# A decoder trunk step on one core: x loaded ahead of c on two queues, the first norm's copy and scale moved, first weight chunks of four tiles

## The chip, the cores and the metric

The kernel runs on one core of one Trainium2 chip. The metric is device time in microseconds (us) of one execution. Before the change it is 1359.24 us, the median of three runs (1358.83 to 1359.36).

## The reference

One step of one decoder layer, for two request groups that share the weights: a prompt of 256 tokens and 8 samples of 4 tokens, together 288 columns (N in the kernel). The width is 2048, so x is 16 tiles of 128 rows by 288 columns. Cut to what matters here:

```
mod = silu(c) @ w_ada + b_ada                  # 6 x 2048 values for each of 9 conditions (1 prompt, 8 samples)
sh1, sc1, g1, sh2, sc2, g2 = split(mod, 6)
h = rmsnorm(x, norm1) * (1 + sc1) + sh1        # rmsnorm: x * rsqrt(mean(x*x) + eps) * g
proj = h @ w_in                                # one input projection for both mixers
...                                            # pooling mixer, Mamba-2 mixer, output projection, gated residual
h2 = rmsnorm(x, norm2) * (1 + sc2) + sh2
ffn = (silu(conv(h2 @ w_gate)) * (h2 @ w_val)) @ w_down
y = rmsnorm(x + g2 * ffn, norm_f)
```

Everything is in float32. The change touches what stands ahead of the input projection and its first chunks: the loads of x and c, the first norm, its modulation and the first weights.

## The kernel before, in words

Features lie on the partitions and the 288 tokens along the free axis. Each large product is done in three matmuls for each weight tile and operand tile (`mm3`, L293): the weight is split into a rounded part `whi` (an ACT cast, L281) and its remainder `wlo` (a VectorE subtraction, L283), the operand likewise into `h1h` and `h1l` (L445, L446), and three of the four cross products are summed. Weights come from one long array, `wflat`, in chunks of up to 1024 columns, in the order in which they are needed. They land in 16 raw buffers (8 + 8); split weights have two buffers of each kind while the input projection begins (SPLIT0, SPLIT1, one each).

The order of work at the start:

- SP issues DMAs in the order c (L182), the four tiles of x (`xa`, L483, four feature tiles each), the first four modulation weights (`raw_ada`, L262), then the first two projection chunks (`raw_xbc`, L924), then further weights as `top_up` asks for them (L269). ACT issues the small constants `early` (L184). DMAs share eight completion semaphores in turn, so each DMA issue first waits for the one eight before it.
- ACT takes silu of c into `sc_c` (L202), for which it first loads a table, then loads the table of the square root by a dummy operation (`warm`, L909).
- The squares of x are taken by ACT (xa0, xa2, L915) and VectorE (xa1, xa3, L917), into a tile with two buffers, and summed over the partitions on TensorE (`ssum`, L919). After each sum two matmuls on the same square tile keep TensorE busy (`warm_pe`, L220 and L921); 14 such matmuls on a tile of ones stand at the very start (L910). From L908 to L945 a manager (`in_order`, L205) pins each of the three engines to the order in which the program names the operations.
- `sqs` (L926) copies the sums out; `rstd_of` (L238) makes the reciprocal root and spreads it over all partitions by a matmul into PSUM (`pbrstd`, L248), and copies that into SBUF (`rstd`, L253). Between these steps run the modulation's matmuls for feature tile 0 (`ada_group_units`, L344), with their copy (`asb`, L329), transpose (L383) and additions (L394, L339).
- `modulate_steps` (L424) makes the projection's operand: x times the norm (L428, from PSUM for feature tile 0, from the SBUF copy for the others), then scale and shift of the prompt's 256 columns (on VectorE at L436, or on ACT at L434 if `act` is set) and of the samples' 32 columns (L441, L442), then cast and remainder (L445, L446).
- The projection runs in seven blocks (BLOCKS, L45), each a range of feature tiles (k) and of output tiles (m). Block 0 is feature tile 0 with all 28 output tiles. `_xbc_chunks` (L79) cuts a block's weights: for block 0 the first chunk has 4 output tiles, the next three have 8. The first two are split by hand ahead of the block (L936 to L943); the third is split by hand and pinned at output tile 3 (L1013), the fourth in `xbc_units` (L621) when it is reached. Each output tile's sum is copied out by ACT or VectorE (L642).

Outside of the pinned parts a scheduler orders each engine's instructions at build time.

Of the kernel before, what the change touches and what calls it, by code (L numbers as in the profile page):

```python
# [14 lines left out]
AF = mybir.ActivationFunctionType  # L15
# [3 lines left out]
P = 128  # L19
D = 2048  # L20
# [4 lines left out]
N = NP + NS  # L25
NC9 = 1 + NB
# [35 lines left out]
KGROUPS = [(0, 1), (1, 1), (2, 2), (4, 4), (8, 4), (12, 4)]  # L62
# [4 lines left out]
RAWC = 1024  # L67
# [11 lines left out]
def _xbc_chunks(bi):  # L79
    (k0, gk), (a, b) = BLOCKS[bi]  # L80
    mper = RAWC // (gk * P)
    cuts = [a, *range(a + (mper // 2 if bi == 0 else mper), b, mper), b]
    return [(list(range(k0, k0 + gk)), list(range(m, n))) for m, n in zip(cuts, cuts[1:])]


# [76 lines left out]
def kernel(ctx: ExitStack, tc, ins, outs):  # L162
    nc = tc.nc
# [13 lines left out]
    def aux(name):  # L177
        return px.tile([P, 512], F32, tag="aux", name=name)


    ct = kp.tile([P, KT, NC9], F32, tag="asb", name="ct")
    nc.sync.dma_start(ct, ins["c"])  # L182
    early = kp.tile([P, NE], F32, name="early")
    nc.scalar.dma_start(early, ins["early"])  # L184
    vec = kp.tile([P, NV], F32, name="vec")
    ident = early[:, K_ID:K_ID + P]
    tri = vec[:, K_TRI:K_TRI + P]
# [11 lines left out]
    bada = early[:, V_BADA:V_BADA + 96].rearrange("p (a k) -> p a k", a=6)  # L199
    sc_c = kp.tile([P, KT, 32], F32, name="sc_c")  # L200
    nc.vector.memset(sc_c, 0.0)
    nc.scalar.activation(sc_c[:, :, 0:NC9], ct, AF.Silu)  # L202

    @contextmanager
    def in_order(*engines):  # L205
# [14 lines left out]
    def warm_pe(n, rhs=None):  # L220

        for _ in range(n):
            nc.tensor.matmul(wps[:, :P], ones, ones if rhs is None else rhs, start=True, stop=True)
# [11 lines left out]
            nc.tensor.matmul(ps[:, c:c + 1], src[:, a:a + P], rhs, start=first and c == 0, stop=last,  # L235
                             skip_group_check=True)

    def rstd_of(ps, n, name, keep=True, mid=None):  # L238

        r3 = kp.tile([P, 3], F32, tag="r3", name="r3" + name)  # L240
        nc.scalar.activation(r3, ps[:, 0:3], AF.Sqrt, bias=epst[:, 0:1], scale=1.0 / n)
        nc.vector.reciprocal(r3, r3)
        if mid:
            mid()
        pb = aux("pb" + name)
        for c, a in enumerate((0, P, N - P)):
            n0 = max(a, c * P)
            nc.tensor.matmul(pb[:, n0:a + P], r3[:, c:c + 1].to_broadcast([P, P]), ident[:, n0 - a:],  # L248
                             start=True, stop=True)
        if not keep:  # L250
            return pb[:, :N], None
        r = kp.tile([P, N], F32, tag="rstd", name=name)
        nc.scalar.copy(r, pb[:, :N])  # L253
        return pb[:, :N], r

# [20 lines left out]
    def fetch(key):  # L276
        return ahead.pop(key)[1]

    def split_steps(raw, a, n, name):
        hi = wp[0].tile([P, RAWC], F32R, tag="whi", name="whi_" + name)  # L280
        yield nc.scalar.copy(hi[:, :n], raw[:, a:a + n])  # L281
        lo = wp[0].tile([P, RAWC], F32R, tag="wlo", name="wlo_" + name)
        yield hi, lo, nc.vector.tensor_tensor(lo[:, :n], raw[:, a:a + n], hi[:, :n].bitcast(F32), ALU.subtract)  # L283

    def split(raw, a, n, name, urgent=True, pin=False):
        with tc.high_priority() if urgent else nullcontext():
            cast, (hi, lo, rest) = split_steps(raw, a, n, name)
        if pin:
            tc.keep_in_program_order(cast)
            tc.keep_in_program_order(rest)  # L290
        return hi, lo
# [7 lines left out]
    ready = {}  # L299
# [124 lines left out]
    def modulate_steps(xv, rstd, which, shp, k0, gk, name, eng=None, act=False):  # L424

        h = kp.tile([P, 4, N], F32, tag="hmod", name="h_" + name, bufs=2)
        hv = h[:, :gk, :]
        nc.vector.tensor_tensor(hv, xv,  # L428
                                rstd.unsqueeze(1).to_broadcast([P, gk, N]), ALU.mult)
        yield  # L430
        for i in range(gk):
            am, sh = amul[:, which, k0 + i, 0:1], ada[:, shp, k0 + i, 0:1]
            if act:
                nc.scalar.activation(h[:, i, 0:NP], h[:, i, 0:NP], AF.Identity, bias=sh, scale=am)  # L434
            else:
                nc.vector.tensor_scalar(h[:, i, 0:NP], h[:, i, 0:NP], am, sh, ALU.mult, ALU.add)  # L436
        hs = hv[:, :, NP:N].rearrange("p k (b l) -> p k b l", b=NB)
        sa = amul[:, which, k0:k0 + gk, 1:NC9].unsqueeze(3).to_broadcast([P, gk, NB, NL])
        sb = ada[:, shp, k0:k0 + gk, 1:NC9].unsqueeze(3).to_broadcast([P, gk, NB, NL])
        eng = eng or nc.gpsimd  # L440
        eng.tensor_tensor(hs, hs, sa, ALU.mult)  # L441
        eng.tensor_tensor(hs, hs, sb, ALU.add)  # L442
        yield
        for i in range(gk):
            nc.scalar.copy(xhi[0][k0 + i], h[:, i, :])  # L445
            nc.vector.tensor_tensor(xlo[0][k0 + i], h[:, i, :], xhi[0][k0 + i].bitcast(F32), ALU.subtract)  # L446
# [33 lines left out]
    xa = []  # L480
    for q in range(4):
        t = mx.tile([P, 4, N], F32, tag="blk", name=f"xa{q}", bufs=4)
        nc.sync.dma_start(t, ins["x"][:, 4 * q:4 * q + 4, :])  # L483
        xa.append(t)

    def xav(k0, gk):
        return xa[k0 // 4][:, k0 % 4:k0 % 4 + gk, :]
# [165 lines left out]
    def drain(gen):  # L653
        for _ in gen:
            pass
# [252 lines left out]
    with in_order(*(e.engine for e in (nc.tensor, nc.scalar, nc.vector))):  # L908
        nc.scalar.activation(warm, sc_c[:, 0, 0:1], AF.Sqrt, scale=0.0)  # L909
        warm_pe(WU[0])  # L910
        ssum = aux("ssum1")
        for q in range(4):
            sq = kp.tile([P, 4, N], F32, tag="hmod", name=f"sq{q}", bufs=2)
            if q % 2 == 0:
                nc.scalar.activation(sq, xa[q], AF.Square)  # L915
            else:
                nc.vector.tensor_tensor(sq, xa[q], xa[q], ALU.mult)  # L917
            for i in range(4):
                nc.tensor.matmul(ssum[32 * i:32 * i + 32, :N], ones[:, 0:32], sq[:, i, :],  # L919
                                 start=(q == 0), stop=(q == 3), tile_position=(0, 32 * i))  # L920
            warm_pe(WU[1], sq[:, 0, 0:P])  # L921
        cond = ada_group_units(0)
        next(cond)
        first = [load(("xbc", 0, ci)) for ci in range(2)]  # L924
        sqs = kp.tile([P, N], F32, tag="xsq", name="sqs", bufs=2)
        nc.vector.tensor_copy(sqs, ssum[:, :N])  # L926
        next(cond)
        ssum = aux("ssum1b")
        col_sums(ssum, sqs, early[:, K_S4:K_S4 + 1], True, True)
        next(cond)  # L930
        rstd1p, rstd1 = rstd_of(ssum, D, "rstd1", mid=lambda: (next(cond), next(cond)))
        mod = modulate_steps(xav(0, KGROUPS[0][1]), rstd1p, 0, 0, 0, KGROUPS[0][1], "g0", nc.vector)
        next(mod)
        next(cond)
        drain(cond)
        parts = [split_steps(t, 0, len(ms) * P, f"xbc0_{i}") for i, (t, (_, ms)) in  # L936
                 enumerate(zip(first, _xbc_chunks(0)))]
        for p in parts:
            next(p)
        next(mod)  # L940
        ready["xbc", 0, 0] = next(parts[0])[:2]
        drain(mod)
        ready["xbc", 0, 1] = next(parts[1])[:2]  # L943
        mod = modulate_steps(xav(*KGROUPS[1]), rstd1, 0, 0, *KGROUPS[1], "g1", nc.vector, True)
        next(mod)  # L945
# [46 lines left out]
    for bi in range(len(BLOCKS)):  # L992
        last = bi + 1 == len(BLOCKS)
        top_up()
        if last:

            wp[0].drop(w0)
            w0_ctx.close()
            sx[0] = mx_ctx.enter_context(tc.tile_pool(name="sx", bufs=1, reuse_waits="tile"))
            hi, lo = split(load(("dt",)), 0, KT * NH, "dt")  # L1000
            ps = pm.tile([P, 512], F32, tag="mm", name="mm_dt")
            for k in range(KT):
                mm3(ps[0:NH, :N], hi, lo, k, xhi[0][k], xlo[0][k], k == 0, k == KT - 1, NH)
            late_states()
            dt_stage(ps)
        elif bi == 4:
            nc.sync.dma_start(vec, ins["vec"])
        elif bi == 5:
            late_loads()
        for i, m in enumerate(xbc_units(bi)):  # L1010
            if not last:
                top_up()
                if (bi, i) == (0, 3):  # L1013
                    ready["xbc", 0, 2] = split(fetch(("xbc", 0, 2)), 0, RAWC, "xbc0_2", pin=True)
                if i in VIS[bi]:
                    next(nxt)
                    top_up()
            else:
                pull(back, 0.5 if m < 20 else RB1) if m >= 9 else None
                pull(adas, RA1 / AY)  # L1020

    late = {}
    n = 0
# [44 lines left out]
    x = ff.tile([P, KT, N], F32, name="x")  # L1068
# [342 lines left out]
```

## Time and profile before

| what | before |
|---|---|
| median of three runs | 1359.24 us |
| the profiled execution: its own time | 1359.61 us |
| its span in the profile | 1357.8 us |
| TensorE matmuls busy | 1342.5 us, 99% |
| VectorE / ScalarE / GpSimd busy | 60% / 43% / 16% |
| mean DMA rate over the span | 238 GB/s |

Times in the profile count from the start of the span. PE is TensorE, PEld its weight loads, DVE VectorE, ACT ScalarE, POOL GpSimd, SP SyncE; SPq and ACTq are their sequencers issuing DMAs. In the rows in order of time the columns are the start, the duration, the engine, the line of the program, the operation with its output and inputs, the count, and in brackets the idle time before it and what ended it. A row of waits gives who waited for whom, then us in total, times, and the longest. A row of stretches gives the stretch, its length, the busy time (and instructions) of PE, PEld, DVE, ACT and POOL, the granted TensorE clock, the DMA share and GB/s. A row of DMA issues gives the count, KB each and the median us to landing. TensorE's weight load and matmul rows of a float32 product appear twice for each matmul.

### The profile page before, as it was taken

How to read it: one execution, taken by the hardware profiler on the slowest of the kernel's cores; microseconds unless marked ns; L12 is line 12 of the kernel's file. 1: busy time of each engine (PE TensorE's matmuls, PEld its weight loads, DVE VectorE, ACT ScalarE, POOL GpSimd, SP SyncE). 2: the span in 40 equal slices, each digit the busy share in tenths (PEclk: the TensorE clock that was granted, in tenths of full speed). 3: DMA queues.
4: the chain of work that ended last, by engine and by line, in shares of the span. 5: the costliest groups of instructions: out<-in, count | busy, mean ns of one | idle time of the engine just before them, and what ended most of it. 6: DMA issues, size and time to landing. Idle time of an engine off the chain costs nothing.

```text
span 1357.8 us, 26226 instructions
## 1 busy us (share of the span) xinstructions
PE 1342.5 (99%) x10557; PEld 1247.4 (92%) x10557; DVE 810.1 (60%) x1349; ACT 578.6 (43%) x908; POOL 221.0 (16%) x428
## 2 busy tenths in 40 slices
PE   9999999999999999999999999999999999999997
PEld 7889988776779889999999999999999999999996
DVE  5775568778564448645565455656654556566543
ACT  5243234587643335534443334443433344434442
POOL 0000002122221213111221001212220011222221
PEclk9999999999999999999999999999999999999998
DMA  9999668877888877777555455555554555555531
GB/s 378 405 408 355 252 216 323 335 263 288 326 302 334 310 265 257 248 293 265 184 182 184 167 176 185 197 193 182 189 178 167 183 191 185 192 200 194 180 117 71
DMA packets 97338, 323.20 MB, mean 238 GB/s; under 512 B 10752, under 2 KB 19904, under 8 KB 97216
## 3 DMA queue, kind: packets, MB, share of 16 engines
q1 hardware_dynamic: 93312, 310.64, 62.8%
q0 software_dynamic: 3184, 9.69, 1.9%
q8 instruction: 83, 1.36, 0.4%
q10 hardware_dynamic: 720, 1.19, 0.2%
q14 instruction: 39, 0.32, 0.1%
HBM read 309.78 MB, written 10.39 MB: 236 GB/s over the span
## 4 chain that ended last, share of the span: by engine, by line
PE 96%; DVE 2%; DMA 1%; ACT 0%; issue 0%; SPq 0%; POOL 0%; DVEq 0%; POOLq 0%; ACTq 0%
PE mm_down L296 7%; PE mm_down L295 7%; PE mm_down L297 7%; PE mm_val L296 6%; PE mm_gate L296 6%; PE mm_gate L295 6%; PE mm_gate L297 6%; PE mm_val L297 6%; PE mm_val L295 6%; PE xbc L295 5%; PE adap L324 5%; PE xbc L296 4%; PE xbc L297 4%; PE mm_out L295 3%; PE mm_out L296 3%; PE mm_out L297 2%
## 5 line engine op out<-in xcount | busy, mean ns | idle before, releaser
L296 PE MATMUL mm_down<-al,whi_down 128*128 128x288 f32 x688 | 202.9, 295 | 0.0
L295 PE MATMUL mm_down<-ah,whi_down 128*128 128x288 f32 x688 | 202.7, 295 | 0.0
L297 PE MATMUL mm_down<-ah,wlo_down 128*128 128x288 f32 x688 | 202.4, 294 | 0.0
L296 PE MATMUL mm_gate<-h2l,whi_gate 128*128 128x288 f32 x640 | 189.1, 296 | 0.0
L296 PE MATMUL mm_val<-h2l,whi_val 128*128 128x288 f32 x640 | 189.1, 295 | 0.0
L297 PE MATMUL mm_val<-h2h,wlo_val 128*128 128x288 f32 x640 | 188.8, 295 | 0.0
L297 PE MATMUL mm_gate<-h2h,wlo_gate 128*128 128x288 f32 x640 | 188.8, 295 | 0.0
L295 PE MATMUL mm_gate<-h2h,whi_gate 128*128 128x288 f32 x640 | 188.7, 295 | 0.0
L295 PE MATMUL mm_val<-h2h,whi_val 128*128 128x288 f32 x640 | 187.9, 294 | 0.0
L283 DVE TENSOR_TENSOR wlo_gate<-raw_gate,whi_gate 128x1024 fp32r<-128x1024 f32 x80 | 97.8, 1225 | 135.4 <-ACT whi_gate L281 135.2
L283 DVE TENSOR_TENSOR wlo_down<-raw_down,whi_down 128x1024 fp32r<-128x1024 f32 x96 | 107.5, 1119 | 116.1 <-ACT whi_down L281 115.0
L281 ACT CAST whi_down<-raw_down 128x1024 fp32r<-128x1024 f32 x96 | 92.4, 962 | 167.3 <-PE mm_down L296 118.0
L281 ACT CAST whi_gate<-raw_gate 128x1024 fp32r<-128x1024 f32 x80 | 83.9, 1051 | 159.5 <-PE mm_gate L296 67.7
L281 ACT CAST whi_val<-raw_val 128x1024 fp32r<-128x1024 f32 x80 | 84.1, 1051 | 126.0 <-issue 103.1
L295 PE MATMUL xbc<-h1h,whi_xbc 128*128 128x288 f32 x448 | 133.0, 301 | 1.2 <-ACT h1h L445 1.2
L296 PE MATMUL xbc<-h1l,whi_xbc 128*128 128x288 f32 x448 | 132.1, 296 | 0.0
L297 PE MATMUL xbc<-h1h,wlo_xbc 128*128 128x288 f32 x448 | 130.8, 297 | 0.0
L295 PEld LDWEIGHTS mm_down<-ah,whi_down 128*128 128x128 f32 x688 | 129.3, 188 | 0.0
L296 PEld LDWEIGHTS mm_down<-al,whi_down 128*128 128x128 f32 x688 | 129.3, 188 | 0.0
L297 PEld LDWEIGHTS mm_down<-ah,wlo_down 128*128 128x128 f32 x688 | 129.1, 188 | 0.0
L295 PEld LDWEIGHTS mm_gate<-h2h,whi_gate 128*128 128x128 f32 x640 | 120.5, 188 | 5.0 <-ACT ah L1176 3.4
L295 PEld LDWEIGHTS mm_val<-h2h,whi_val 128*128 128x128 f32 x640 | 120.5, 188 | 0.0
(323 smaller groups left out, 2979.3 us busy)
## 6 DMA issues: line engine op xcount, KB each, us to landing
raw_adap<-wflat SPq DMA_DIRECT2D x128, 512.0 KB, 5.5
raw_gate<-wflat SPq DMA_DIRECT2D x80, 512.0 KB, 3.5
raw_val<-wflat SPq DMA_DIRECT2D x80, 512.0 KB, 3.6
raw_ada<-wflat SPq DMA_DIRECT2D x64, 512.0 KB, 9.7
raw_xbc<-wflat SPq DMA_DIRECT2D x51, 512.0 KB, 8.9
raw_down<-wflat SPq DMA_DIRECT2D x48, 512.0 KB, 3.5
raw_out<-wflat SPq DMA_DIRECT2D x32, 512.0 KB, 6.6
raw_down<-wflat SPq DMA_DIRECT2D x32, 384.0 KB, 3.0
```

What stands on the lines that cost most here:

```text
L281: yield nc.scalar.copy(hi[:, :n], raw[:, a:a + n])
L283: yield hi, lo, nc.vector.tensor_tensor(lo[:, :n], raw[:, a:a + n], hi[:, :n].bitcast(F32), ALU.subtract)
L295: nc.tensor.matmul(ps, whi[:, w], bh, start=first, stop=False)
L296: nc.tensor.matmul(ps, whi[:, w], bl, start=False, stop=False)
L297: nc.tensor.matmul(ps, wlo[:, w], bh, start=False, stop=last)
L324: nc.tensor.matmul(ps[32 * j:32 * j + 32, :nb], sc_c[:, k, :], raw[:, c:c + nb], start=(k == 0), stop=(k == KT - 1), tile_position=(0, 32 ...
```

## The change

- The tiles of x are loaded first, xa0 and xa2 by SP and xa1 and xa3 by ACT; the loads of c and of `early` and the silu of c are written behind them.
- The first norm's copy to SBUF is written behind feature tile 0's cast and remainder; until then its PSUM form alone is used.
- For feature tile 0, ACT scales and shifts the prompt's columns instead of VectorE.
- Block 0's weights are cut into chunks of 4, 4, 4, 8 and 8 output tiles instead of 4, 8, 8 and 8; the third, fourth and fifth are split by hand and pinned at output tiles 3, 7 and 13.

```
 def _xbc_chunks(bi):
-    cuts = [a, *range(a + (mper // 2 if bi == 0 else mper), b, mper), b]
+    cuts = [a, *([4, 8] if bi == 0 else []), *range(a + (12 if bi == 0 else mper), b, mper), b]
...
-    nc.sync.dma_start(ct, ins["c"])
-    nc.scalar.dma_start(early, ins["early"])
...
-    nc.scalar.activation(sc_c[:, :, 0:NC9], ct, AF.Silu)
...
-    def rstd_of(ps, n, name, keep=True, mid=None):
+    def rstd_of(ps, n, name, keep=True, mid=None, later=False):
...
         r = kp.tile([P, N], F32, tag="rstd", name=name)
+        if later:
+            return pb[:, :N], lambda: (nc.scalar.copy(r, pb[:, :N]), r)[1]
         nc.scalar.copy(r, pb[:, :N])
...
-        nc.sync.dma_start(t, ins["x"][:, 4 * q:4 * q + 4, :])
+        (nc.scalar if q % 2 else nc.sync).dma_start(t, ins["x"][:, 4 * q:4 * q + 4, :])
         xa.append(t)
+    nc.sync.dma_start(ct, ins["c"])
+    nc.scalar.dma_start(early, ins["early"])
+    nc.scalar.activation(sc_c[:, :, 0:NC9], ct, AF.Silu)
...
-        rstd1p, rstd1 = rstd_of(ssum, D, "rstd1", mid=lambda: (next(cond), next(cond)))
-        mod = modulate_steps(xav(0, KGROUPS[0][1]), rstd1p, 0, 0, 0, KGROUPS[0][1], "g0", nc.vector)
+        rstd1p, rstd1 = rstd_of(ssum, D, "rstd1", mid=lambda: (next(cond), next(cond)), later=True)
+        mod = modulate_steps(xav(0, KGROUPS[0][1]), rstd1p, 0, 0, 0, KGROUPS[0][1], "g0", nc.vector, True)
...
         ready["xbc", 0, 0] = next(parts[0])[:2]
         drain(mod)
+        rstd1 = rstd1()
...
-                if (bi, i) == (0, 3):
-                    ready["xbc", 0, 2] = split(fetch(("xbc", 0, 2)), 0, RAWC, "xbc0_2", pin=True)
+                if bi == 0 and i in (3, 7, 13):
+                    ci = {3: 2, 7: 3, 13: 4}[i]
+                    ready["xbc", 0, ci] = split(fetch(("xbc", 0, ci)), 0, len(_xbc_chunks(0)[ci][1]) * P,
+                                                f"xbc0_{ci}", pin=True)
```

As built, ACT still issues the load of `early` ahead of its two tiles of x.

## The prediction

> **What bounds the kernel now.** I read the page first (busy times, then the chain that ended last), then TensorE's waits, then the instructions in order of time over the first 20 us.
>
> ```profile
> span 1357.8 us, 26226 instructions
> PE 1342.5 (99%) x10557; PEld 1247.4 (92%) x10557; DVE 810.1 (60%) x1349; ACT 578.6 (43%) x908; POOL 221.0 (16%) x428
> PE 96%; DVE 2%; DMA 1%; ACT 0%; issue 0%; SPq 0%; POOL 0%; DVEq 0%; POOLq 0%; ACTq 0%
> ...
> PE xbc L295 <- ACT h1h L445: 1.2, 2, 0.9
> ...
> PE pool L877 <- DVE pout L872: 0.7, 1, 0.7
> ```
>
> TensorE is busy 99% of the span and holds 96% of the chain. The two wait rows are the largest of two stretches, 19 to 200 us and from there to the end: after the first projection matmul TensorE hardly waits, and never for a DMA. So whatever moves that first matmul moves the end by the same amount; no slack behind it can take up a delay, and a DMA that runs further ahead buys nothing. The question is when the first projection matmul starts. Before, that is 19.22 us, and these rows lead to it (start, duration, engine, what it waited for):
>
> ```profile
> 3.03 1.28 ACT L202 ACT_TABLE_LOAD   x1 [3.03 <-DMA ct<-c]
> 4.33 0.34 ACT L202 ACTIVATE sc_c<-ct 128x144 f32<-128x144 f32 x1
> 4.68 1.28 ACT L909 ACT_TABLE_LOAD   x1
> 5.97 0.20 ACT L909 ACTIVATE warm<-sc_c 128x1 f32<-128x1 f32 x1
> 6.08 1.15 ACT L915 ACTIVATE sq<-xa 128x1152 f32<-128x1152 f32 x1
> 8.78 1.16 ACT L915 ACTIVATE sq<-xa 128x1152 f32<-128x1152 f32 x1 [1.55 <-DMA xa<-x]
> ...
> 7.29 1.36 DVE L917 TENSOR_TENSOR sq<-xa 128x1152 f32<-128x1152 f32 x1 [5.57 <-DMA xa<-x]
> 10.24 1.36 DVE L917 TENSOR_TENSOR sq<-xa 128x1152 f32<-128x1152 f32 x1 [1.59 <-DMA xa<-x]
> 12.41 0.46 DVE L926 COPY sqs<-ssum 128x288 f32<-128x288 f32 x1 [0.81 <-PE ssum L919]
> ...
> 7.28 0.69 PE L919 MATMUL ssum<-sq,ones 128*32 128x288 f32 x8 [0.59 <-ACT sq L915]
> 9.99 0.69 PE L919 MATMUL ssum<-sq,ones 128*32 128x288 f32 x8
> 10.62 0.71 PE L223 MATMUL warm<-sq,ones 128*128 128x128 f32 x4
> 11.65 0.69 PE L919 MATMUL ssum<-sq,ones 128*32 128x288 f32 x8 [0.32 <-DVE sq L917]
> 19.22 0.80 PE L295 MATMUL xbc<-h1h,whi_xbc 128*128 128x288 f32 x4 [0.86 <-ACT h1h L445]
> ```
>
> Two things are to be seen. The x tiles land at 7.29, 8.78 and 10.24 us, and squares and sums follow them. And ACT's first square stands behind four instructions, the first of which, a table load, waits for c: from c at 3.03 to the square at 6.08 it is **3.05 us**. Before, this hides behind the transfer of the first x tile.
>
> **The change part by part.**
>
> *Loading x ahead of c.* In the list of the changed kernel as built, SP issues xa0, xa2, then c, then the weights; ACT issues early (still first), xa1, xa3. ACT's order behind that is unchanged: table load (waiting for c's DMA), silu, table load, warm, square of xa0, square of xa2. So ACT's squares now wait for a c that stands behind two tiles on its own queue. When does it land?
>
> ```profile
> GB/s 0 0 176 272 209 412 393 393 424 430 399 428 418 415 415 415 415 415 385 421 396 399 426 399 382 415 426 393 410 421 404 399 431 399 393 431 415 393 432 393
> ...
> xa<-x SPq DMA_DIRECT2D x4, 576.0 KB, 6.1
> early<-early ACTq DMA_DIRECT2D x1, 152.5 KB, 2.4
> ct<-c SPq DMA_DIRECT2D x1, 72.0 KB, 2.2
> ```
>
> The first row is the rate in slices of 0.75 us: from 3.75 us on, one queue alone moves about 410 GB/s, the plateau that lasts. If SP's queue were served first, c would land when two tiles, c and early have passed, the bytes behind the landing at 7.29; if ACT's tiles all pass too, 10.24. Large tiles first may also spare part of the slow start: the slices of 176, 272 and 209 lose (236+140+203)/412 x 0.75 = 1.05 us against 412. With two queues side by side, c is nearly the last of the five: I take **9.5 us** (10.24 less half of that loss and a little), ends 7.3 and 10.2.
>
> The Trainium skill, page "DMA: Bandwidth & Descriptors", sections "Queues, rings and completion order" and "Rules for kernel authors", speaks against this step: engines take packets in turn from the queues with work, each queue in its own order, and spreading loads over SP and ACT saves issue time, not bandwidth. By that rule c lands beside xa3, near the upper end, and the sum would be up to 0.7 us larger; the plateau on one queue agrees with it.
>
> ACT then: 9.5 + 3.05 = 12.55, first square to 13.7, and the first sum on TensorE starts at 13.75 instead of 7.28. The two extra DMA issues on ACT, and SP's two fewer, are hidden in ACT's wait.
>
> *What waits behind it.* TensorE runs the sums in order, and the square tile has two buffers: the square of xa2 waits until sum and warm matmuls of xa0 are done, that of xa3 (VectorE) for those of xa1. Before, loads spaced these out; now they make a staircase. And TensorE stands idle from the end of its first warm matmuls to 13.75:
>
> ```profile
> 1.06 5.63 PE L223 MATMUL warm<-ones 128*128 128x128 f32 x28 [1.06 <-DVE ones L192]
> ...
> 2.71 1.70 PE L223 MATMUL warm<-ones 128*128 128x128 f32 x7
> ...
> 5.70 0.99 PE L223 MATMUL warm<-ones 128*128 128x128 f32 x7
> ...
> 1347.15 0.85 PE L248 MATMUL pbrstdf<-early,r3rstdf 128*128 128x128 f32 x6
> ...
> 1350.00:1350.40 0.40, 0.00 (x0) 0.00 (x0) 0.40 (x2) 0.00 (x0) 0.00 (x0) 1.00 0.74 242
> 1350.40:1350.70 0.30, 0.00 (x0) 0.00 (x0) 0.30 (x2) 0.00 (x0) 0.00 (x0) 0.89 0.07 19
> 1350.70:1351.00 0.30, 0.00 (x0) 0.00 (x0) 0.30 (x2) 0.00 (x0) 0.00 (x0) 0.50 0.37 131
> ```
>
> Seven warm matmul rows take 1.70 us early and 0.99 us from 5.70 on: TensorE starts slow and is quick some 4.6 us after its first matmul. After the last one (ended 1348.0) the granted clock, the third figure from the right, falls from 1.00 to 0.50 at about 1350.6, 2.6 us later. The idle time now is 13.75 - 6.69 = 7.1 us, so TensorE should come back slow, by 1.70/0.99 = 1.7, until about 13.75 + 4.6 = 18.35. A sum with its warm matmuls takes 10.62 + 0.71 - 9.99 = 1.34 us quick, 2.2 slow.
>
> The Trainium skill, page "TensorE: Matmul & The Clock Gate", Part 1, has the clock halve after an idle window of about 3.4 us and return after a busy one, counted freely. By that rule the return comes 3.4 to 6.8 us after the restart, which makes the sum up to 1 us smaller or larger; the fall after 2.6 us agrees with halving, and is a little earlier.
>
> The staircase, slow: xa0's sum and warm 13.75 to 15.95; xa1's (its square long done) to 18.15; xa2's (square 16.0 to 17.15) mostly quick, 18.15 to 19.5; square of xa3 18.2 to 19.55, sum from 19.6; the copy of the sums, which came 0.76 after that sum began (12.41 - 11.65), at 20.35. Before: 12.41. **+7.9 us.**
>
> *The norm's copy and the scale on ACT.* From the sums' copy to the first projection matmul it is 6.81 us before:
>
> ```profile
> 15.29 0.38 PEld L370 LDWEIGHTS adag<-raw_ada,sc_c 128*32 128x32 f32 x16 [0.23 <-DMA raw_ada<-wflat]
> ...
> 15.87 0.85 PE L248 MATMUL pbrstd<-early,r3rstd 128*128 128x128 f32 x6
> ...
> 17.19 0.45 DVE L428 TENSOR_TENSOR h_g<-xa,pbrstd 128x288 f32<-128x288 f32 x1 [2.36 <-ACT rstd L253]
> 17.76 0.17 DVE L339 SCALAR_TENSOR_TENSOR amul<-ada,early 128x9 f32<-128x9 f32 x1
> 18.74 0.43 ACT L445 CAST h1h<-h_g 128x288 fp32r<-128x288 f32 x1
> L434 ACT ACTIVATE h_g<-h_g,ada,amul x15: 586/588/604, 31.7 to 177.9; 128x256 f32<-128x256 f32 x15
> ```
>
> Three waits shrink. The modulation's weights will long have landed: -0.23. The multiply at 17.19 waited for ACT's copy of the norm; in the list of the changed kernel it waits for the norm's matmuls alone, which end at 15.87 + 0.85 = 16.72: -0.45. From amul to the cast took 0.98 us (17.76 to 18.74) over VectorE's scale and two small operations; now ACT scales (0.59) beside those two, 0.2 + 0.59 = 0.79: -0.2. Together **-0.9 us**. The copy moved behind the first cast delays only later copies, which wait for the projection's first sums a microsecond later anyway; were that cover gone it would cost its 0.40. ACT's casts of the first two weight chunks stand ahead of the scale, and are smaller now; they fit behind the modulation's copy.
>
> *Chunks of four tiles.* Bytes and matmuls stay. But there are two buffers of split weights, so the third chunk's cast (ACT) and remainder (VectorE) must fit behind the tiles of the second.
>
> ```profile
> 19.86 0.29 PE L296 MATMUL xbc<-h1l,whi_xbc 128*128 128x288 f32 x1
> 19.99 0.30 PE L297 MATMUL xbc<-h1h,wlo_xbc 128*128 128x288 f32 x1
> ...
> 21.15 1.05 ACT L281 CAST whi_xbc<-raw_xbc 128x1024 fp32r<-128x1024 f32 x1
> ...
> 22.50 1.22 DVE L283 TENSOR_TENSOR wlo_xbc<-raw_xbc,whi_xbc 128x1024 fp32r<-128x1024 f32 x1
> ```
>
> Matmuls follow each other by 0.13, three to a tile: eight tiles cover 3.1 us, against 1.05 + 1.22 = 2.3 for a chunk of eight, 0.8 to spare. Four tiles cover 1.6, against 1.1 for a chunk of four, 0.5 to spare, and copies of the sums of about the same length as before stand between on both engines, 0.8 us or so: the third remainder comes about 0.3 us late. I take **+0.3**, ends 0 and 1. The added DMA issue on SP costs nothing: TensorE is late, so weights are early.
>
> **Sum.** 7.9 - 0.9 + 0.3 = **+7.3 us** on the profiled execution's 1359.61 us (span 1357.8): 1366.9. The median of the three runs, 1359.24, lies 0.4 lower: **1366.5 us.**
>
> **The rivals.**
> 1. *c comes in time, not slower.* If c's small packets passed the tiles and landed by about 3 us, as now, nothing would hold ACT; the point from which it decides is a landing before 10.24 - 1.16 - 3.05 = 6 us or so. Then what is left is the -0.9, and up to 1.05 us from the earlier start of x: 1357.3 to 1358.4, say 1358. Against it: c is third on its queue, and on SP the four x tiles landed one after the other. Chance 0.08.
> 2. *c as late as I say, but TensorE's clock stays up.* Then four quick stairs: sums' copy at about 18.5, 6.1 late, and 6.1 - 0.9 + 0.3 = +5.5: 1364.7. For it: my switch rests on two places of one trace. Against: 7.1 us is far over 2.6. Chance 0.17.
> 3. *SP's queue is served first*, c at 7.3: all 2.2 us earlier, TensorE still idle 4.9 us and slow: +5.1, 1364.3. For it: ACT issues xa1 only after early. Chance 0.2.
> 4. *The small chunks starve the split buffers*: the third and fourth chunks each late by a whole cast and remainder of four tiles, 1.1 more: 1367.6. Chance 0.07.
> My own forecast has the rest, 0.48.
>
> **How the numbers follow.** The range runs from below rivals 2 and 3 together (+3.2, 1362.4) to the sum with c at its upper end and the buffers late (+8.9, 1368.1): 1362.2 to 1368.4. It leaves out rival 1 and an error of the staircase I have not seen. About 0.2%, 2.7 us, is what a measurement of this kernel can tell from no change. Rival 1 lies within it, with a small part beyond; all other cases are slower by more. Faster 0.03, same 0.08, slower 0.89.
>
> **What would show it.** After: ACT's first table load waiting for c until 8 to 10 us; TensorE idle from 6.7 to 12 or 14; the four sums in a row with slow warm matmuls between; sums' copy near 20; first projection matmul near 26; from there on the same rhythm as before. VectorE's first multiply no longer waits for ACT's copy. Wrong, if ACT's first square starts with the first landed x tile, or if TensorE finds time back later, in waits that I read as absent.

## The result, and the profile after

The changed kernel takes 1366.09 us (median of six runs, 1365.22 to 1366.76) against 1359.30 us before (six runs): a ratio of 1.0049, 95% interval 1.0036 to 1.0062, so 0.5% slower. The profiled execution took 1366.01 us, 6.4 more than that of before. From the page after:

```profile
span 1364.2 us, 26235 instructions
PE 1343.6 (98%) x10557; PEld 1248.1 (91%) x10557; DVE 811.8 (60%) x1349; ACT 578.4 (42%) x910; POOL 219.9 (16%) x428
```

TensorE has 1.1 us more of busy time and 6.4 us more of span: most of the difference is idle time, and the rows show it at the start. ACT's instructions there, in order of time (line numbers of the changed kernel):

```profile
9.86 1.28 ACT L486 ACT_TABLE_LOAD   x1 [9.86 <-DMA ct<-c]
11.16 0.34 ACT L486 ACTIVATE sc_c<-ct 128x144 f32<-128x144 f32 x1
11.51 1.28 ACT L911 ACT_TABLE_LOAD   x1
12.81 0.20 ACT L911 ACTIVATE warm<-sc_c 128x1 f32<-128x1 f32 x1
12.92 1.15 ACT L917 ACTIVATE sq<-xa 128x1152 f32<-128x1152 f32 x1
16.54 1.16 ACT L917 ACTIVATE sq<-xa 128x1152 f32<-128x1152 f32 x1 [2.48 <-issue]
```

c lands at 9.86 us instead of 3.03, and the same 3.06 us of silu and tables follow before the first square. The second square waits for its buffer, until the sum and the warm matmuls of the first are done. TensorE and VectorE over the same stretch:

```profile
14.12 1.19 PE L921 MATMUL ssum<-sq,ones 128*32 128x288 f32 x8 [7.60 <-ACT sq L917]
15.23 1.22 PE L220 MATMUL warm<-sq,ones 128*128 128x128 f32 x4
16.39 1.19 PE L921 MATMUL ssum<-sq,ones 128*32 128x288 f32 x8
17.50 1.22 PE L220 MATMUL warm<-sq,ones 128*128 128x128 f32 x4
18.66 0.87 PE L921 MATMUL ssum<-sq,ones 128*32 128x288 f32 x8
19.46 0.71 PE L220 MATMUL warm<-sq,ones 128*128 128x128 f32 x4
20.18 0.69 PE L921 MATMUL ssum<-sq,ones 128*32 128x288 f32 x8
...
27.07 0.80 PE L294 MATMUL xbc<-h1h,whi_xbc 128*128 128x288 f32 x4 [0.35 <-ACT h1h L444]
```

```profile
8.38 1.36 DVE L919 TENSOR_TENSOR sq<-xa 128x1152 f32<-128x1152 f32 x1 [6.67 <-DMA xa<-x]
18.77 1.36 DVE L919 TENSOR_TENSOR sq<-xa 128x1152 f32<-128x1152 f32 x1 [9.03 <-PE warm L220]
20.94 0.46 DVE L928 COPY sqs<-ssum 128x288 f32<-128x288 f32 x1 [0.81 <-PE ssum L921]
```

VectorE took the square of xa1 at 8.38, and its sum waits on TensorE until 16.39, in order behind that of xa0. Ahead of the last square, of xa3, VectorE is idle for 9.03 us; what ends it are the warm matmuls that still read the square's buffer. The first two sums with their warm matmuls take 2.27 us each (from 14.12 to 16.39 to 18.66), the last 1.27 (TensorE's next operation starts at 21.45). The granted clock (third figure from the right) in stretches shows why:

```profile
6.00:8.00 2.00, 0.51 (x5) 0.32 (x3) 0.00 (x0) 0.00 (x0) 0.00 (x0) 1.00 1.03 415
8.00:10.00 2.00, 0.00 (x0) 0.00 (x0) 1.36 (x1) 0.14 (x1) 0.00 (x0) 0.71 1.05 419
10.00:12.00 2.00, 0.00 (x0) 0.00 (x0) 0.00 (x0) 1.97 (x3) 0.00 (x0) 0.50 1.02 408
...
16.00:18.00 2.00, 2.00 (x13) 0.86 (x12) 0.00 (x0) 1.16 (x1) 0.00 (x0) 0.50 1.04 410
18.00:20.00 2.00, 2.00 (x16) 1.16 (x15) 1.23 (x1) 0.00 (x0) 0.00 (x0) 0.73 1.02 406
20.00:22.00 2.00, 1.99 (x30) 1.05 (x28) 0.58 (x2) 0.00 (x0) 0.00 (x0) 1.00 1.04 416
```

TensorE's warm matmuls ended at 6.52; the clock is halved within the stretch from 8 to 10 us and back within that from 18 to 20. All the while the DMA engines move 406 to 419 GB/s (the last column), from about 10 us on only weights, which nobody can use yet.

Behind the sums' copy the way is shorter, 6.13 us (27.07 - 20.94) instead of 6.81. First VectorE's rows, then ACT's:

```profile
25.12 0.46 DVE L427 TENSOR_TENSOR h_g<-xa,pbrstd 128x288 f32<-128x288 f32 x1 [1.76 <-PE pbrstd L245]
25.49 0.17 DVE L393 TENSOR_TENSOR ada<-adat_g,early 128x18 f32<-128x18 f32 x1
25.69 0.17 DVE L338 SCALAR_TENSOR_TENSOR amul<-ada,early 128x9 f32<-128x9 f32 x1
```

```profile
25.96 0.60 ACT L433 ACTIVATE h_g<-h_g,ada,amul 128x256 f32<-128x256 f32 x1 [0.29 <-DVE amul L338]
26.59 0.43 ACT L444 CAST h1h<-h_g 128x288 fp32r<-128x288 f32 x1
```

The multiply now follows the norm's matmuls, and the scale runs on ACT beside VectorE's two small operations.

### The profile page after: what moved, and what is told of

It reads as the page before. It is cut to its first block, busy times and chain, and to the rows that moved or that the text cites. A ratio compares the mean times of both kernels' runs of the same rounds, so it can differ in the third digit from the quotient of the medians.

```text
span 1364.2 us, 26235 instructions
## 1 busy us (share of the span) xinstructions
PE 1343.6 (98%) x10557; PEld 1248.1 (91%) x10557; DVE 811.8 (60%) x1349; ACT 578.4 (42%) x910; POOL 219.9 (16%) x428
## 4 chain that ended last, share of the span: by engine, by line
PE 96%; DVE 2%; ACT 0%; issue 0%; POOL 0%; DVEq 0%; POOLq 0%; ACTq 0%
PE mm_down L295 7%; PE mm_down L294 7%; PE mm_down L296 7%; PE mm_val L295 6%; PE mm_gate L295 6%; PE mm_gate L294 6%; PE mm_val L296 6%; PE mm_gate L296 6%; PE mm_val L294 6%; PE xbc L294 5%; PE adap L323 5%; PE xbc L296 4%; PE xbc L295 4%; PE mm_out L294 3%; PE mm_out L295 3%; PE mm_out L296 2%
```

## The experiments

Theory A was that c's place behind x in its queue costs all that is lost, by holding ACT, while the other parts are a small gain. Rivals were that another part costs too (B), that the slow clock is most of it (C), and later that something in the change gave time back further on (F). "Faster" and "slower" are against the kernel before, run on the same chip beside each.

**The loads of before, the rest of the change kept.**

```
+    nc.sync.dma_start(ct, ins["c"])            # again ahead of x; early and silu too
...
-        (nc.scalar if q % 2 else nc.sync).dma_start(t, ...)
+        nc.sync.dma_start(t, ...)
```

> The changed kernel with the loads of before: c first, all of x on SP, silu of c ahead of x. Theory A (c behind x holds ACT's squares; everything else of the change is a small gain): sums' copy back at 12.4 us, first projection matmul at about 18.5 (0.7 earlier than before), the later waits as in the changed kernel, 1 to 1.4 us less: 1357 to 1358 us. Rival B (the moved copy, the scale on ACT or the small chunks cost something too, and c explains less than 8.5 us): 1360 or more.

1359.21 us against 1359.74 before (ratio 0.9996, interval 0.9987 to 1.0005). With the loads undone the loss is gone. The expected total was missed by 1.2 us: the first projection matmul came at 19.23, since in this execution x landed half a microsecond later (sums' copy at 12.91), and the later waits were not the short ones of the changed kernel, which the experiment on a late start explains.

**The new loads, ACT's squares ahead of silu and tables.**

```
+            # behind the loop over the four tiles of x, not ahead of it:
+        nc.scalar.activation(sc_c[:, :, 0:NC9], ct, AF.Silu)
+        nc.scalar.activation(warm, sc_c[:, 0, 0:1], AF.Sqrt, scale=0.0)
```

> The changed kernel with its loads (x first on two queues, c behind), but on ACT the silu of c and both table loads stand behind the squares. Only the wait is taken from the squares' way; c lands as late as before in the changed kernel. Theory A: sums' copy at about 13 us, paced by xa1 and xa3 on ACT's queue (landed 8.4 and about 10 us), first projection matmul at about 19, total 1357.5 to 1359. Rival (x on two queues is itself what is late, or TensorE idles anyway): still above 1363.

1359.83 us against 1359.74 (1.0001, 0.9992 to 1.0010). What lands when is nearly the same (c 7.8 us after its issue, 8.1 in the changed kernel), only the wait was taken from the squares' way, and 6 us returned; the total is 0.8 above the range that was expected. ACT's rows:

```profile
5.04 1.16 ACT L915 ACTIVATE sq<-xa 128x1152 f32<-128x1152 f32 x1 [1.61 <-DMA xa<-x]
8.41 1.16 ACT L915 ACTIVATE sq<-xa 128x1152 f32<-128x1152 f32 x1 [2.21 <-PE warm L220]
9.59 1.28 ACT L922 ACT_TABLE_LOAD   x1
10.89 0.34 ACT L922 ACTIVATE sc_c<-ct 128x144 f32<-128x144 f32 x1
11.24 1.28 ACT L923 ACT_TABLE_LOAD   x1
```

The square of xa0 starts at 5.04, a microsecond sooner than before (6.08, behind the tables), but that of xa1 from the other queue only at 8.02 (7.29 before), and the sums' copy comes at 12.98, no sooner than the 12.41 of before. Loading x on two queues ahead of c buys nothing at the end of the norm even when c is not in the way.

**The new loads alone, in the kernel before.**

```
-    nc.sync.dma_start(ct, ins["c"])            # and early, and silu of c
...
-        nc.sync.dma_start(t, ins["x"][...])
+        (nc.scalar if q % 2 else nc.sync).dma_start(t, ins["x"][...])
+    nc.sync.dma_start(ct, ins["c"])            # and early, and silu of c
```

> The kernel before with the new loads alone. Theory A: the whole loss and none of the gains: sums' copy at about 20.9 us, first projection matmul 8 to 8.5 later than before: 1367 to 1368. Rival B: about as the changed kernel or below, 1366 or less.

1366.95 us against 1359.74 (1.0053, 1.0039 to 1.0066): the whole loss without the rest of the change, though a little less than theory A had it (1367 to 1368). The sums' copy came at 20.42 and the first projection matmul at 27.07, 7.9 later than before and not 8 to 8.5; the clock came back at 18.01 here, a microsecond sooner than in the changed kernel (19.07).

**c behind x on one queue**, no other edit: c's load and silu are written behind the loop over x, all tiles on SP.

> The kernel before with one thing moved: c's load from the head of SP's queue to behind the four x tiles, all on SP; no second queue, no other edit. Theory A (c's place in its queue is the cause, not the two queues): ACT's first table load waits until 9 to 10 us, sums' copy at about 20, total 1366 to 1367. Rival B (the two queues together delay c): c lands by 8 and the total stays below 1364.

1366.84 us against 1359.56 (1.0054, 1.0039 to 1.0069).

```profile
10.15 1.28 ACT L484 ACT_TABLE_LOAD   x1 [10.15 <-DMA ct<-c]
```

c lands at 10.15 here and at 9.86 on two queues: the second queue is not the cause. It is one move of one small load. The sums' copy came at 21.35, over a microsecond later than expected, and the total where it was expected, for the slow sums and the time given back later weigh against each other here too.

**x on two queues, c ahead of it**: the loads of c and early back at the top of the changed kernel.

> The changed kernel with x still on two queues, but c ahead of x on SP and early ahead of it on ACT (ACT issues its second tile only behind the silu). Theory A: c lands near 3 us as before, the loss is gone: 1359 to 1359.6, as with the old loads. Rival B (two queues are what is slow): above 1362.

1359.58 us against 1359.56 (1.0000, 0.9991 to 1.0008). The second queue neither costs nor gains in this order of loads.

**TensorE kept busy until the first sum.**

```
-WU = (14, 2, 2, 2, 6)
+WU = (46, 2, 2, 2, 6)
```

> The changed kernel with 46 instead of 14 warm matmuls at the start, so that TensorE is idle for only half a microsecond or so ahead of the first sum, and not for 7.6. Theory A with the clock as one term: granted clock stays at 1.00, the four sums take 1.3 each in a staircase, sums' copy at about 18.9 instead of 20.9: 1364 us. Rival C (the slow clock is most of the loss): below 1362. Rival D (the clock plays no part): 1366, and more if the warm matmuls run over.

1363.87 us, 2.2 less than the changed kernel's 1366.09, still slower than before (1.0031, 1.0019 to 1.0042). The rows of the sums' copy and of the clock:

```profile
18.81 0.46 DVE L928 COPY sqs<-ssum 128x288 f32<-128x288 f32 x1 [0.81 <-PE ssum L921]
```

```profile
6.00:14.00 8.00, 7.96 (x71) 7.77 (x70) 1.36 (x1) 4.16 (x5) 0.00 (x0) 1.00 1.03 413
14.00:20.00 6.00, 5.88 (x65) 3.20 (x66) 1.82 (x2) 1.16 (x1) 0.00 (x0) 1.00 1.03 399
```

c landed when it did (9.75), the clock stayed at 1.00, and the sums' copy came 2.1 us sooner. So the slow clock is about 2 us of the loss (by the totals of the profiled executions 1.8, by the medians, each against the kernel before beside it, 2.7), and a consequence of the wait, not a cause of its own: rivals C and D both fall.

**The norm's part alone** (`later=True`, ACT's scale for tile 0, and the call behind the first remainder).

> The kernel before with the norm's copy behind the first cast and the prompt's scale on ACT, alone. Theory A: from the sums' copy to the first projection matmul 6.2 to 6.3 us instead of 6.8, nothing else moves: 0.5 us faster than before, 1358.8 to 1359.2. Rival: the copy, now late, holds the second feature tile's multiply and the gain is lost in the next 10 us: no difference.

1359.43 us against 1359.60 (1.0001, 0.9992 to 1.0010): not to be told from no change. Its profiled execution was the slowest of its eleven (1362.54 us) and shows a limit of this order:

```profile
16.65 0.62 ACT L283 CAST whi_xbc<-raw_xbc 128x512 fp32r<-128x512 f32 x1
19.40 1.05 ACT L283 CAST whi_xbc<-raw_xbc 128x1024 fp32r<-128x1024 f32 x1 [2.12 <-DMA raw_xbc<-wflat]
20.35 0.60 ACT L436 ACTIVATE h_g<-h_g,ada,amul 128x256 f32<-128x256 f32 x1
```

The prompt's scale now stands on ACT behind the second chunk's cast, and when that chunk lands late the first projection matmul, here at 21.47, waits for a weight that it doesn't need. TensorE stood idle for 2.62 us ahead of it, and that was enough for the clock: it was granted at 0.50 from 21.05 to 24.46, and projection matmuls took 0.44 us in place of 0.29. The expected 6.2 to 6.3 us to the first projection matmul could not be seen in this execution. Why the chunk landed late in it is not shown.

**The chunks alone** (`_xbc_chunks` and the splits at output tiles 3, 7 and 13).

> The kernel before with block 0's chunks of 4, 4, 4, 8 and 8 tiles, alone. Theory A: the first projection matmul where it was; one wait of 0.2 to 0.3 us in the 10 us behind it (seen in the experiment with the old loads, 6.7 us behind the first matmul): same to 0.3 slower. Rival: the smaller first cast brings the first matmul forward: faster.

1360.26 us against 1359.60 (1.0004, 0.9995 to 1.0012): no difference that this measurement resolves. A wait of 0.25 us stands 6.7 us behind the first projection matmul, as expected; the median is 0.7 above that of before, where 0 to 0.3 was expected.

**A late start in the kernel before.**

```
+        warm_pe(36)
         cond = ada_group_units(0)
```

> The kernel before with 36 more warm matmuls behind the sums, about 8 us, so that the projection starts late while nothing of the loads, of ACT or of the clock changes. Theory E (a late start gives back about 1.1 us in the projection's first blocks, since weights and modulation are then ahead): first matmul at about 27.2, the stretch from there to the dt product 166 instead of 167 us, total 1366 to 1366.6. Rival F (the changed loads or the new chunks gave the 1.1 us back): the stretch stays at 167, total 1367.5 or more.

1366.27 us against 1359.60 (1.0050, 1.0037 to 1.0062). Loads, ACT's order and chunks are those of before; only TensorE is late. The first projection matmul starts at 27.46, 8.2 us later than before, and the end is only 6.7 later. Where the dt product starts, at the end of the projection's first six blocks, is a landmark; its row before, after, and here (the last pair of times is the first and last start):

```profile
L295 PE MATMUL mm_dt<-h1h,whi_dt x16: 290/293/295, 186.3 to 192.2; 128*24 128x288 f32 x16
```

```profile
L294 PE MATMUL mm_dt<-h1h,whi_dt x16: 290/292/295, 193.0 to 198.9; 128*24 128x288 f32 x16
```

```profile
L295 PE MATMUL mm_dt<-h1h,whi_dt x16: 290/292/295, 193.3 to 199.2; 128*24 128x288 f32 x16
```

From the first projection matmul to there it is 167.1 us before, 165.9 after and 165.8 here. The old loads, with a first matmul at 19.23 and this product at 186.5, keep 167.3, though they have all the other parts of the change. It is so in every trace: the five kernels whose projection starts between 24.95 and 27.99 us need 165.8 to 166.0 for this stretch, the seven that start between 18.45 and 19.38 need 166.7 to 167.6, whatever their loads, norm and chunks. Only the profiled execution of the norm's part alone stands outside, with 168.0 and a halved clock at its start. So the 1.1 us come back wherever the projection starts late, and rival F falls. One wait of which they are made, from the kernel before:

```profile
45.68 0.30 PE L297 MATMUL xbc<-h1h,wlo_xbc 128*128 128x288 f32 x1
46.34 0.79 PE L295 MATMUL xbc<-h1h,whi_xbc 128*128 128x288 f32 x4 [0.36 <-ACT h1h L445]
```

From one start to the next it is 0.66 us where 0.13 is usual, so this wait alone is half of the 1.1, and it is a wait for an operand that ACT casts, not for weights. After, no wait of TensorE for an operand is listed between the first projection matmul and the dt product but the first one's own. The stretch holds the same 1593 matmuls in all these kernels, so no work was moved out of it, and all but 0.1 us of the difference arises in its first 30 us. A late start also changes the built order, in which the modulation's next matmuls stand earlier; how much is that and how much the weights' and the modulation's being ahead was not separated.

**Meant to beat both: x, then c, on one queue, squares first, the norm's part, old chunks.**

> Meant to beat both: the kernel before with x first on SP alone, c behind it, ACT's squares ahead of silu and both tables, and the norm's copy and scale as changed; chunks as before. Theory A: x without c and early ahead of it lands 0.5 to 1 us sooner and in order, sums' copy at 11.5 to 12, silu and tables fit ahead of the root: first projection matmul at 17.7 to 18.3, 1358 to 1358.6 us. Rival: c, landing near 10, now holds the modulation's matmuls, or x comes no sooner: no gain over the norm's part alone.

1359.96 us against 1359.60 (1.0005, 0.9995 to 1.0014): no gain. Its eleven executions spread from 1358.29 to 1361.97, four of them above 1361; the profiled one took 1359.07. There the sums' copy did come sooner, at 11.84, and the first projection matmul only at 18.90:

```profile
16.84 1.05 ACT L280 CAST whi_xbc<-raw_xbc 128x1024 fp32r<-128x1024 f32 x1 [0.44 <-DMA raw_xbc<-wflat]
17.79 0.59 ACT L433 ACTIVATE h_g<-h_g,ada,amul 128x256 f32<-128x256 f32 x1
```

The second chunk's landing holds the scale again. That the four longest executions are those in which it landed later still, as in the profiled one of the norm's part alone, is likely and not shown.

**The same with the chunks of 4, 4, 4, 8 and 8.**

> As the kernel that loads x and then c on one queue with the squares first, and with the chunks of 4, 4, 4, 8 and 8 tiles. There ACT's cast of the second chunk (512 KB) waited for its DMA until 16.84 us and held the scale behind it, 0.8 us. With a second chunk of half the size: no such wait, first projection matmul at 17.9 to 18.2 instead of 18.9, one wait of 0.25 behind it: 1358.6 to 1359.2 us. Rival: the weights' landing holds the first matmul all the same, no gain.

1358.68 us against 1359.56 (0.9994, 0.9986 to 1.0003).

```profile
15.96 1.14 ACT L280 CAST whi_xbc<-raw_xbc 128x512 fp32r<-128x512 f32 x2
17.34 0.60 ACT L433 ACTIVATE h_g<-h_g,ada,amul 128x256 f32<-128x256 f32 x1 [0.24 <-DVE amul L338]
```

Both casts now run without a wait, the scale waits for its own operand only, and the first projection matmul starts at 18.45, 0.8 us sooner than before, though not at the expected 17.9 to 18.2. This is the lowest median measured, 7.4 us below the changed kernel; against the kernel before, the interval still holds no change. What the small chunks changed is less the usual execution than the spread: the two profiled executions have spans of 1357.1 us with them and 1356.7 without, but all eleven now lie between 1358.41 and 1359.06, as far as executions on two chips can be compared. They help not TensorE, but ACT's queue, in which a cast stands ahead of the scale.

## Why the prediction was right, point by point

The forecast was 1366.5 us, the measurement 1366.09. The mechanism is the one that was named, and four experiments show it: moving c alone makes the loss, moving c back (with one queue or two) or taking its wait out of the squares' way removes it. But the closeness of the total is in part luck, for errors of both signs met:

| step | predicted | measured |
|---|---|---|
| c lands | 9.5 us | 9.86 |
| clock slow again, and until | yes, to 18.35 | yes, to about 19 |
| sums' copy, later than before | +7.9 | +8.53 |
| sums' copy to first projection matmul | -0.9 | -0.68 |
| small chunks | +0.3 | 0 (a wait of 0.25 with an early start) |
| given back in the projection | 0 | -1.1 |
| dt product to the end of the span | 0 | -0.3 |
| profiled execution | +7.3 | +6.4 |

- *c's landing.* The lower bound, SP's queue served first, is refuted; c came at 9.86, near the upper bound of 10.2. The sum took 0.74 us off 10.24 because large tiles first would spare part of the slow start, and they spared none: up to 3.75 us the rate in slices of 0.75 us is 108, 126 and 325 GB/s now, which loses 1.23 us against 412, where it was 1.05. What put c 0.38 us ahead of 10.24 is not shown. The rule that the prediction names from the Trainium skill, page "DMA: Bandwidth & Descriptors", section "Queues, rings and completion order", had put c near that upper end, and this trace agrees with it.
- *The staircase* stands in the trace as written. A slow sum with its warm matmuls took 2.27 us (2.2 predicted, where 1.34 times 1.7 is 2.3), the clock fell 2.3 us after the last matmul (2.6 predicted), and returned 4.95 us after the restart (4.6 predicted). That the sums' copy came 0.6 later than predicted is these terms and c's 0.36.
- *The norm's part.* The weights' wait gave 0.17 and the multiply's 0.43; the scale on ACT gave 0.08 and not 0.2: it started 0.27 us after amul (25.69 to 25.96), a longer step than the 0.2 that was allowed.
- *The step that failed* is "no slack behind it can take up a delay, and a DMA that runs further ahead buys nothing". It was read from the largest wait row of each stretch. Of the 1.1 us that came back, those rows list 0.36 as a wait of TensorE; the rest lies in matmuls that follow each other more slowly than by 0.13. Behind 200 us TensorE's listed waits add up to 2.2 us, and not to the 0.7 of the row shown. A kernel with an added delay and no other edit gives back as much.
- *The small chunks.* Their wait exists, of the size predicted, but only when the projection starts early. And the prediction missed their benefit: "they fit behind the modulation's copy" took the casts' weights as landed, and with a chunk of 512 KB ahead of the scale they are not always.
- *The range.* By the prediction's own terms its ends would be 7.3 - 1.8 - 2.2 = +3.3 and 7.3 + 0.7 + 1.1 = +9.1 us, not +3.2 and +8.9; the measured +6.8 (of the medians) lies well within either.
- *Rivals.* Rival 2, the clock staying up, is what the experiment with more warm matmuls made: 1363.9 against the 1364.7 it was priced at. Rivals 1 and 3 fall with c's landing at 9.86, rival 4 with the missing wait for the small chunks.

## What to carry to other kernels

Before a small load is moved behind large ones, look up which engine waits for it and what stands behind that wait in the engine's own order: here the wait for 72 KB held a table load, with it two squares, and with them TensorE. A long wait at one engine can cost twice, once as itself and once as the slow clock on which TensorE returns (2 of the 6.8 us here). And a delay at the start was not carried to the end in full (8.2 us at the first projection matmul, 6.7 at the end): what starts sooner meets waits that lateness covers, like the small chunks' 0.25 us, so a part of a change that is worth half a microsecond should be measured with a late and an early start.

## What the runs showed of the hardware that was not expected

- A load's place in the issue order moved its landing by 7 us: 72 KB landed at 3.03 us at the head of a queue, 9.86 behind two tiles of 576 KB with two more on the other queue, and 10.15 behind four on its own.
- The wait for c stood ahead of the table load, and so its 1.28 us came behind c's landing. That is how this program was built, and not so for every table load: with a square as ACT's first operation, the square's table load ran at 1.19 us and only the square itself waited for its tile, until 5.35 (x, then c, on one queue with small chunks). In the traces silu waits for two things: for VectorE's zeroing of `sc_c` on the operation itself, for c on a semaphore instruction of its own, which stands ahead of the table load (9.81 us in the changed kernel). The square carries its one wait itself. That silu's table load would run early if it had one wait less was not tried.
- The clock's fall does not keep a fixed distance from the last matmul. It came 2.3 us behind it in the changed kernel, 2.7 with c behind x on one queue, 5.2 with the new loads alone, and 2.2 with the norm's part alone, where the whole pause was 2.62 us. From fall to return it was 10.24, 10.24, 6.82 and 3.41 us, in all four a multiple of 3.41 within the reading. (The times are worked out from the granted clock of half-microsecond stretches: 0.83 over 8.50 to 9.00 puts the changed kernel's fall at 8.83.)
